# One core of Trainium2: the low half of the queries times the high half of the keys alone, as two 64-partition products

## The chip, the core and the metric

The kernel runs on one core of one Trainium2 chip, in one launch. The metric is the device time of that core in microseconds, lower is better. A run's time is the median of several executions; the profile is one further execution, recorded by the hardware profiler.

## The reference, cut to what matters

One layer of a hybrid decoder trunk over 2048 positions of width 1024: a modulated RMS norm, one combined projection `W_in` whose columns feed three groups of heads, an output projection with a residual, and a convolutional feed-forward block (1024 to 2 x 2816 to 1024) with another. One of the three groups is attention with a forget bias, 8 heads of 64; the others are a chunkwise mLSTM and a spatial gating unit. The change touches the scores of the attention alone:

```python
qa = rms_norm(to_heads(q_a, N_ATTN_HEADS), g_q).transpose(0, 2, 1, 3)
ka = rms_norm(to_heads(k_a, N_ATTN_HEADS), g_k).transpose(0, 2, 1, 3)
...
for blk in range(s_len // Q_BLOCK):              # 16 blocks of 128 queries
    lo, hi = blk * Q_BLOCK, (blk + 1) * Q_BLOCK
    logits = (jnp.einsum('bhtd,bhsd->bhts', q[:, :, lo:hi], k[:, :, :hi]) * scale
              + F[:, :, lo:hi, None] - F[:, :, None, :hi])
    logits = jnp.where(mask, logits, -jnp.inf)
    p = jax.nn.softmax(logits, axis=-1)
    outs.append(jnp.einsum('bhts,bhsd->bhtd', p, v[:, :, :hi]))
```

All inputs and the output are float32.

## The kernel before

**Split numbers.** Products are taken in the type float32r. To come near float32 each operand is split into a high half (the value copied into float32r) and a low half (what that copy lost). Most products of the kernel are `mm3` (lines 53 to 56): high times high, high times low, low times high. The scores do it otherwise: a head has 64 features, so the 64 high and the 64 low features of the keys fill the 128 partitions of one tile, and one product over 128 partitions gives the query's one half times both halves of the key.

**Stages.** By the clock of the profiled execution, the norms, the projections and the mLSTM run until about 690 us, the attention from there to about 1140 us, the output projection and the feed-forward block after it. The first scores of head 0 lie beside the last products of the projections (`acc`, L54 to L56). While attention runs, the projections' results come back from DRAM scratch: `k_d` and `q_d` hold for each pair of heads a high and a low block of 128 features (two heads of 64) by 2048 positions.

**Attention.** `load_k(h)` fills the tile `kk` of a head: partitions 0 to 63 the high halves of its keys, 64 to 127 the low halves, each by one DMA of 64 rows of 8 KB (L157). The forget bias `nf` (broadcast to all partitions) and the values follow. `load_q(h, tb, tag)` loads for 512 queries two tiles: `q2[0]` holds the high halves twice (on partitions 0 to 63 and again on 64 to 127), `q2[1]` the low halves twice (L173).

`scores` runs over the four blocks of 128 queries in 512, and for each over its keys in parts of up to 1024, one PSUM tile `sp` each (two buffers). Each part is one or two blocks of up to 512 keys. For each block two products over 128 partitions add into the same place (L206): `q2[0]` with `kk`, which is high times high plus high times low, and `q2[1]` with `kk`, which is low times high plus low times low. In the last block of a row a product of an identity with a mask (L210, bf16) adds the causal mask. Then one DVE instruction (L212) adds the bias, takes the row's extreme into `nm` and writes the tile `L`; ACT takes the exponentials (L223), GpSimd scales the rows (L225 to L228).

`finish` turns the weights on TensorE, four tiles of 128 by 128 at a time (`tp`, L259), splits them on ACT (`phi`, L262) and DVE (`plo`, L263), and multiplies them with the values (`op`, L245 and L246); ACT copies the result out (L250).

**Order.** `phase` puts the score parts of one step of 512 queries beside the `finish` of the step before, some parts of one, some of the other. The framework then orders each engine's instructions itself, so that on TensorE score products stand among transposes and value products. Keys and values of the next head are asked for after the first of a head's four steps; the queries of a step one step ahead. All loads go through the queue of SP, in order. L393, which the prediction uses, is a small transpose of parameter rows at the start of the kernel.

**Counts.** A head has 40 blocks of keys (4 + 8 + 12 + 16 for the four steps), so 640 products of L206 in all, and 128 mask products.

Of the kernel before, what the change touches and what calls it, by code (L numbers as in the profile page):

```python
# [8 lines left out]
F32 = mybir.dt.float32  # L9
# [8 lines left out]
P = 128  # L18
# [15 lines left out]
def trunk(  # L34
# [7 lines left out]
    V, A, G, T = nc.vector, nc.scalar, nc.gpsimd, nc.tensor  # L42
    dma = nc.sync.dma_start
# [19 lines left out]
    k_d = dr.tile([NH // 2, 2, P, S], F32, name="k_d")  # L63
# [32 lines left out]
    identb = cst.tile([P, P], BF16, name="identb")  # L96
    V.tensor_copy(identb, ident)
    maskb = cst.tile([P, P], BF16, name="maskb")
# [52 lines left out]
    def load_k(h):  # L151
        tag, e = "kvA" if h == 0 else "kvB", slice(h % 2 * 64, h % 2 * 64 + 64)
        kk = pool.tile([P, S], F32R, name="kk", tag=tag)
        nf = pool.tile([P, S], F32, name="nf", tag=tag)
        vv = pool.tile([P, S // P, P], F32R, name="vv", tag=tag)
        for i in range(2):
            dma(kk[64 * i : 64 * i + 64].bitcast(F32), k_d[h // 2, i, e])  # L157
        dma(nf, nf_d[h : h + 1, :].broadcast_to([P, S]))
        kv[h] = kk, nf, vv

# [21 lines left out]
    def l_tile(h, tb, c, w):  # L182
        if h and (tb == 0 or (tb, c) == (2, 1)) or (h, tb, c) == (0, 2, 1):
            tag = "L2"
        else:
            n_l[0] += 1
            tag = "LA" if h < NH - 2 and (n_l[0] - 1) % 20 < 8 else "LB"
        return pool.tile([P, w], F32, name="L", tag=tag)

    def scores(h, tb, q2, rows):  # L190

        kk, nf, _ = kv[h]
        for i in range(4):
            n_s = (tb * 4 + i + 1) * P
            parts = [(s0, min(1024, n_s - s0)) for s0 in range(0, n_s, 1024)]
            qs = slice(i * P, (i + 1) * P)

            nm = pool.tile([P, 2], F32, name="nm", tag="nm")
            L = []
            for c, (s0, w) in enumerate(parts):  # L200
                sp = pp.tile([P, 1024], F32, name="sp", tag="sp")
                for b in range(0, w, 512):
                    bw = min(512, w - b)
                    last = s0 + b + bw == n_s
                    for n in range(2):
                        T.matmul(  # L206
                            sp[:, b : b + bw], q2[n][:, qs], kk[:, s0 + b : s0 + b + bw], start=n == 0, stop=n == 1 and not last
                        )
                    if last:
                        T.matmul(sp[:, w - P : w], identb, maskb, start=False, stop=True)  # L210
                L.append(l_tile(h, tb, c, w))
                V.tensor_tensor_reduce(  # L212
                    out=L[c], in0=sp[:, :w], in1=nf[:, s0 : s0 + w], scale=-1.0, scalar=3.0e38 if c == 0 else nm[:, 0:1],
                    op0=ALU.add, op1=ALU.min, accum_out=nm[:, c : c + 1],
                )
                yield
            rows.append(L)
            rs = pool.tile([P, 2], F32, name="rs", tag="rs")

            def exps(L=L, nm=nm, rs=rs):  # L220
                n = len(L)
                for c in range(n):
                    A.activation(L[c], L[c], AF.Exp, bias=nm[:, n - 1 : n], scale=-1.0, accum_out=rs[:, c : c + 1])  # L223
                if n == 2:
                    G.tensor_tensor(rs[:, 0:1], rs[:, 0:1], rs[:, 1:2], op=ALU.add)  # L225
                G.tensor_tensor(rs[:, 0:1], rs[:, 0:1], mone, op=ALU.pow)
                for t in L:
                    G.tensor_scalar(t, t, rs[:, 0:1], 1.0, op0=ALU.mult, op1=ALU.mult)  # L228

            exps()  # L230
# [38 lines left out]
    def phase(now, then, lead=0):  # L269

        rows = []
        sc, n_sc = iter(()), 0
        if now:
            sc, n_sc = scores(*now, kv.pop(now) if now in kv else load_q(*now, "qB"), rows), (4, 4, 8, 8)[now[1]]
            if now in order and now != order[-1]:
                nxt = order[order.index(now) + 1]
                kv[nxt] = load_q(*nxt, "qB")
        n_fin = sum(4 * (t[1] + 1) for t in then)
        fin = (u for t in then for u in finish(*t))
        done = 0  # L280
        for n in range(n_sc):
            next(sc)
            while done < (n + 1 - lead) * (n_fin - 5) // (n_sc - lead):
                next(fin)
                done += 1
        for _ in sc:
            pass
        for _ in fin:
            pass
        return now and [(*now, rows)]  # L290
# [471 lines left out]
    def use_qk(which):  # L762
        def go(tt, ps):
            sq = pool.tile([P, 512], F32, name="qsq", tag="sq")
            A.activation(sq, ps, AF.Square)
            ss = pool.tile([P, 8], F32, name="ss", tag="ss")
            V.tensor_reduce(ss, sq.rearrange("p (h d) -> p h d", h=8), axis=AX.X, op=ALU.add)
            V.tensor_scalar(ss, ss, 1.0 / 64, EPS, op0=ALU.mult, op1=ALU.add)
            rsqrt(ss, 8)

            def normal():
                n = pool.tile([P, 8, 64], F32, name="qn", tag="q2k")
                V.tensor_tensor(n, ps.rearrange("p (h d) -> p h d", h=8), bc(ss, 2, 64), op=ALU.mult)
                after(3, lambda: turn(tt, n))

            after(1, normal)

        def turn(tt, n):
            tp = tr_ps()
            for j in range(4):  # L780
                T.transpose(tp[:, j * P : (j + 1) * P], n[:, 2 * j : 2 * j + 2].rearrange("p e d -> p (e d)"), ident)
            g, d = (gq8, q_d) if which == "q" else (gk, k_d)
            hi = pool.tile([P, 512], F32R, name="qhi", tag="qhl")
            lo = pool.tile([P, 512], F32R, name="qlo", tag="qhl")
            A.activation(hi, tp, AF.Copy, scale=g)
            V.scalar_tensor_tensor(lo, tp, g, hi.bitcast(F32), op0=ALU.mult, op1=ALU.subtract)
            for e, t in enumerate((hi, lo)):
                dma(
                    d[:, e, :, tt * P : (tt + 1) * P].rearrange("h p t -> p h t"),
                    t.bitcast(F32).rearrange("p (h t) -> p h t", h=4),  # L790
                )

        return go
# [125 lines left out]
    def mlstm(qi):  # L919
# [133 lines left out]
    blocks = [  # L1053
        ([(C_KM, 256), (C_G, 16)], nat(use_km)),
        ([(C_QM, 256), (C_VM + 256, 256)], do_qo),
        ([(C_VM, 256)], nat(use_vm)),
        ([(C_US, 512)], nat(use_sgu)),
        ([(C_K, 512)], nat(use_qk("k"))),
        ([(C_Q, 512)], nat(use_qk("q"))),
        ([(C_V, 512)], nat(use_v)),  # L1060
    ]
# [9 lines left out]
    for n, (half, i) in enumerate(steps):  # L1071
# [7 lines left out]
        if n == len(steps) - 1:  # L1079
            while background:  # L1080
                if next(background[0], True):
                    background.pop(0)
            n_accs[0] = 2
            pool.close("proj_r")
            pp.close("proj_r")
            attention_open_right()

            load_k(0)
            first_rows = [], []
            first = [scores(0, tb, load_q(0, tb, "qA"), r) for tb, r in zip((1, 0), first_rows)]  # L1090
            load_v(0, (0, 1))
            background += first
# [23 lines left out]
    last = [(0, 1, first_rows[0]), (0, 0, first_rows[1])]  # L1116
    order = [(h, tb) for h in range(NH) for tb in (TBS if h == NH - 1 else (2, 3) if h == 0 else range(4))]
    for h in range(NH):
        for n, tb in enumerate(TBS if h == NH - 1 else (2, 3) if h == 0 else range(4)):
            if (h, n) == (NH - 2, 1):  # L1120
                pool.close("att_r")
                wout_open_right()
            if (h, n) == (NH - 2, 3):
                load_w(0)
            last = phase((h, tb), last, 3 if (h, n) == (0, 0) else 0)
            if n == 0 and h < NH - 1:
                load_k(h + 1)
                load_v(h + 1, range(4))
# [607 lines left out]
```

## Time and profile before

| | |
|---|---|
| time, median of 3 runs (lowest, highest) | 2624.97 us (2623.48, 2627.48) |
| the profiled execution's own time | 2626.13 us |
| its span | 2624.1 us |
| PE, PEld busy | 2537.4 us, 2101.5 us |
| DVE, ACT, POOL busy | 2004.4 us, 1274.2 us, 399.0 us |
| DMA | 379.58 MB, mean 145 GB/s |
| mean granted clock of TensorE | 0.992 |

Engines: PE is TensorE's matmul, PEld its weight load (overlaps PE), DVE VectorE, ACT ScalarE, POOL GpSimd, SP the engine whose queue issues the DMAs. L206 is line 206 of the kernel. The recorded ends of matmuls are modelled and lie behind the start of the next one, so a product's cost in a steady run is the distance of two starts and not its duration. A timeline row has start and duration in us, the engine, the line, the operation, result and operands, shapes, and in brackets the idle time before it with what ended it ("issue": nothing that the profile shows). A row of the grouped lines has the busy time in us and the mean duration in ns behind the first bar, the idle time before it with what ended it behind the second.

### The profile page before, as it was taken

Reading aid. Unit: us, or ns where it says so; the run is one execution under the profiler, and the core shown is the slowest. Engines: PE = TensorE matmul, PEld = TensorE weight load, DVE = VectorE, ACT = ScalarE, POOL = GpSimd, SP = SyncE. Lnnn points to the kernel's source line nnn. Section 1 sums busy time; section 2 is a strip of 40 time slices with the busy share of each in tenths; the row PEclk is TensorE's granted clock in tenths of the full one; section 3 lists DMA queues with packets and bytes.
Section 4 is the critical chain, followed back from the end, with each engine's and each line's share of the span. In section 5 each row is a group of like instructions: output and inputs, shape, how many; then the busy total and the mean of one; then the engine's idle time right before and its main releaser. Section 6 shows DMA issues by size and latency. Waiting matters only on the chain.

```text
span 2624.1 us, 36472 instructions
## 1 busy us (share of the span) xinstructions
PE 2537.4 (97%) x12521; PEld 2101.5 (80%) x12537; DVE 2004.4 (76%) x3438; ACT 1274.2 (49%) x2424; POOL 399.0 (15%) x532
## 2 busy tenths in 40 slices
PE   5999999999999999999989999999999999999999
PEld 4887878878787887777768888888888888888787
DVE  7856646455378888866769888888888887898797
ACT  4333334333278888854555444444444444444443
POOL 2012210032246656620000000000000000000000
PEclk9999999999999999999999999999999999999999
DMA  7564653334564445257723222246222227658533
GB/s 248 173 185 132 194 153 111 116 88 131 165 177 113 114 136 165 65 162 238 274 65 105 89 81 84 86 160 225 81 88 81 87 66 256 233 166 295 186 95 117
DMA packets 302592, 379.58 MB, mean 145 GB/s; under 512 B 31934, under 2 KB 194588, under 8 KB 300360
## 3 DMA queue, kind: packets, MB, share of 16 engines
q1 hardware_dynamic: 302408, 377.26, 45.4%
q8 instruction: 99, 1.62, 0.3%
q14 instruction: 85, 0.70, 0.1%
HBM read 276.44 MB, written 100.74 MB: 144 GB/s over the span
## 4 chain that ended last, share of the span: by engine, by line
PE 76%; DVE 10%; DMA 5%; ACT 3%; issue 3%; POOL 2%; SPq 1%; DVEq 0%; ACTq 0%; POOLq 0%
PE ub L56 10%; PE ub L55 10%; PE ub L54 10%; PE acc L54 5%; PE acc L56 5%; PE acc L55 5%; PE db L55 4%; PE db L56 4%; PE db L54 4%; PE sp L206 3%; PE tp L259 3%; PE wps L55 2%; PE wps L54 2%; PE wps L56 2%; PE op L245 2%
## 5 line engine op out<-in xcount | busy, mean ns | idle before, releaser
L54 PE MATMUL acc<-wh,hh 128*128 128x512 f32 (+2 forms) x768 | 288.2, 376 | 4.3 <-DVE ev L688 2.3
L54 PE MATMUL ub<-T,wsph 128*128 128x512 f32 x704 | 274.2, 390 | 5.8 <-ACT wsph L1348 5.8
L56 PE MATMUL acc<-wh,hl 128*128 128x512 f32 (+2 forms) x768 | 275.7, 362 | 0.8 <-DVE hl L563 0.5
L55 PE MATMUL acc<-wl,hh 128*128 128x512 f32 (+2 forms) x768 | 275.3, 360 | 0.3 <-DVE wl L593 0.3
L56 PE MATMUL ub<-T,wspl 128*128 128x512 f32 x704 | 273.7, 389 | 0.6 <-DVE wspl L1349 0.6
L55 PE MATMUL ub<-T,wsph 128*128 128x512 f32 x704 | 273.9, 389 | 0.0
L55 PE MATMUL db<-wspl,wsph 128*128 128x512 f32 x616 | 240.2, 390 | 2.6 <-DVE wspl L1480 2.6
L56 PE MATMUL db<-wsph,wspl 128*128 128x512 f32 x616 | 239.6, 389 | 0.0
L54 PE MATMUL db<-wsph 128*128 128x512 f32 x616 | 238.2, 389 | 0.3 <-ACT wsph L1479 0.3
L1348 ACT CAST wsph<-S 128x512 fp32r<-128x512 f32 x176 | 109.7, 623 | 227.7 <-PE ub L55 159.1
L263 DVE TENSOR_TENSOR plo<-tp,phi 128x512 fp32r<-128x512 f32 (+1 forms) x320 | 186.9, 607 | 31.6 <-ACT phi L262 29.4
L54 PE MATMUL ub<-B,wsph 128*128 128x512 f32 x528 | 207.1, 392 | 2.8 <-ACT wsph L1348 2.8
L56 PE MATMUL ub<-B,wspl 128*128 128x512 f32 x528 | 207.0, 392 | 0.7 <-DVE wspl L1349 0.7
L55 PE MATMUL ub<-B,wsph 128*128 128x512 f32 x528 | 206.8, 392 | 0.0
L223 ACT ACTIVATE L<-L,nm 128x1024 f32<-128x1024 f32 (+2 forms) x192 | 172.5, 902 | 35.7 <-DVE nm L212 34.4
L259 PE MATMUL tp<-ident,L 128*128 128x128 f32 x1088 | 177.0, 274 | 2.6 <-POOL L L228 0.8
L262 ACT CAST phi<-tp 128x512 fp32r<-128x512 f32 (+1 forms) x320 | 159.9, 520 | 40.5 <-PE tp L259 38.9
L206 PE MATMUL sp<-kk,q 128*128 128x512 f32 (+3 forms) x640 | 169.3, 375 | 3.2 <-DVE nm L212 2.2
L1479 ACT CAST wsph<-act 128x512 fp32r<-128x512 f32 x132 | 82.2, 623 | 178.9 <-PE db L55 161.0
L228 POOL TENSOR_SCALAR L<-L,rs 128x1024 f32<-128x1024 f32 (+2 forms) x192 | 167.2, 880 | 11.0
L54 PEld LDWEIGHTS acc<-wh,hh 128*128 128x128 f32 x768 | 147.1, 192 | 24.2 <-DVE ev L688 2.7
L56 PEld LDWEIGHTS acc<-wh,hl 128*128 128x128 f32 x768 | 146.0, 191 | 23.1 <-DVE hl L563 1.3
(339 smaller groups left out, 5936.2 us busy)
## 6 DMA issues: line engine op xcount, KB each, us to landing
w<-in_w_up_dram SPq DMA_DIRECT2D x88, 512.0 KB
wd<-in_w_down_dram SPq DMA_DIRECT2D x176, 256.0 KB
wa<-in_w_ada_dram SPq DMA_DIRECT2D x96, 256.0 KB
act_d<-yc SPq DMA_DIRECT2D x44, 512.0 KB
act<-act_d SPq DMA_DIRECT2D x44, 512.0 KB
wr<-in_w_in_dram SPq DMA_DIRECT2D x64, 256.0 KB
q<-q_d SPq DMA_DIRECT2D x128, 128.0 KB
hc_d<-hl SPq DMA_DIRECT2D x28, 512.0 KB
```

Source lines behind the costliest of these rows:

```text
L54: T.matmul(ps, lh, rh, start=start, stop=False, skip_group_check=resume)
L55: T.matmul(ps, lh, rl, start=False, stop=False, skip_group_check=resume)
L56: T.matmul(ps, ll, rh, start=False, stop=stop, skip_group_check=resume)
L206: T.matmul(sp[:, b : b + bw], q2[n][:, qs], kk[:, s0 + b : s0 + b + bw], start=n == 0, stop=n == 1 and not last)
L223: A.activation(L[c], L[c], AF.Exp, bias=nm[:, n - 1 : n], scale=-1.0, accum_out=rs[:, c : c + 1])
L228: G.tensor_scalar(t, t, rs[:, 0:1], 1.0, op0=ALU.mult, op1=ALU.mult)
L245: T.matmul(op[:, c0:], vv[:, j, :], hi[:, c0:], start=(j == 0), stop=False)
L259: T.transpose(tp[:, i * P : (i + 1) * P], rows[i][j // 8][:, (j % 8) * P : (j % 8 + 1) * P], ident)
L262: A.copy(hi[:, c0:], tp[:, c0:])
L263: V.tensor_tensor(lo[:, c0:], tp[:, c0:], hi[:, c0:].bitcast(F32), op=ALU.subtract)
L1348: A.copy(hi, src)
L1479: A.copy(hi, v)
```

## The change

Three things change, all for the product of the query's low half.

- The low half of the query is multiplied with the high half of the key alone. Low times low is no longer computed where a part has two blocks.
- So this product needs 64 partitions. Where a part has two blocks of keys, the first block's product uses partitions 0 to 63 and the second's 64 to 127. For this the key tile is stored otherwise: in every odd block of 512 keys the low half lies on partitions 0 to 63 and the high half on 64 to 127. The product with `q2[0]`, which holds the high half on both, gives the same sum in either order. `load_k` takes four DMAs for it instead of two, each of 64 rows with two runs of 2 KB. A part with a single block keeps its product over 128 partitions.
- The order within a part: the first products of both blocks, then the mask, then the second products.

In the built program 256 of the 640 products run on 64 partitions (128 on each half), declared as products of a 64 by 128 part of the array; the other 384 and all else stay at 128 by 128.

```diff
@@ load_k
+        halves = lambda t: t.rearrange("p (a b c) -> p a b c", b=2, c=512)
         for i in range(2):
-            dma(kk[64 * i : 64 * i + 64].bitcast(F32), k_d[h // 2, i, e])
+            for b in range(2):
+                dma(halves(kk[64 * i : 64 * i + 64].bitcast(F32))[:, :, b, :], halves(k_d[h // 2, i ^ b, e])[:, :, b, :])
@@ scores
                 sp = pp.tile([P, 1024], F32, name="sp", tag="sp")
-                for b in range(0, w, 512):
-                    bw = min(512, w - b)
-                    last = s0 + b + bw == n_s
-                    for n in range(2):
-                        T.matmul(
-                            sp[:, b : b + bw], q2[n][:, qs], kk[:, s0 + b : s0 + b + bw], start=n == 0, stop=n == 1 and not last
-                        )
-                    if last:
-                        T.matmul(sp[:, w - P : w], identb, maskb, start=False, stop=True)
+                blocks = [(b, min(512, w - b)) for b in range(0, w, 512)]
+                last = s0 + w == n_s
+                for b, bw in blocks:
+                    T.matmul(sp[:, b : b + bw], q2[0][:, qs], kk[:, s0 + b : s0 + b + bw], start=True, stop=False)
+                if last:
+                    T.matmul(sp[:, w - P : w], identb, maskb, start=False, stop=False)
+                for n, (b, bw) in enumerate(blocks):
+                    r = slice(64 * n, 64 * n + 64) if len(blocks) == 2 else slice(0, P)
+                    T.matmul(sp[:, b : b + bw], q2[1][r, qs], kk[r, s0 + b : s0 + b + bw], start=False, stop=True)
```

## The prediction

> **What bounds the kernel now.** I read the page first, for the bound of the whole span, then the attention stage alone, since only it changes. The products of L206 run from 694.5 us to 1134.0 us (durations, then first and last start); I take 690 to 1140 us as the stage.
>
> ```profile
> L206 PEld LDWEIGHTS sp<-kk,q x640: 186/188/247, 694.5 to 1133.8; 128*128 128x128 f32 x160
> L206 PE MATMUL sp<-kk,q x640: 218/393/504, 694.7 to 1134.0; 128*128 128x512 f32 x127, 128*128 128x128 f32 x17, 128*128 128x384 f32 x16
> ```
>
> The page:
>
> ```profile
> span 2624.1 us, 36472 instructions
> PE 2537.4 (97%) x12521; PEld 2101.5 (80%) x12537; DVE 2004.4 (76%) x3438; ACT 1274.2 (49%) x2424; POOL 399.0 (15%) x532
> PE 76%; DVE 10%; DMA 5%; ACT 3%; issue 3%; POOL 2%; SPq 1%; DVEq 0%; ACTq 0%; POOLq 0%
> ```
>
> TensorE is busy for 97% of the span and carries 76% of the chain that ended last. In the stage, the windows view (span of the window, then busy time of PE, PEld, DVE, ACT, POOL, then the granted clock) and the grouped lines of PE say the same:
>
> ```profile
> 45.00:48.00 3.00, 2.70 (x10) 1.96 (x10) 2.97 (x9) 2.11 (x4) 1.99 (x4) 0.50 1.00 403
> 690.00:1140.00 450.00, 437.95 (x2614) 354.27 (x2612) 362.54 (x726) 345.52 (x757) 255.01 (x388) 1.00 0.47 132
> ```
>
> ```profile
> L259 PE MATMUL tp<-ident,L 128*128 128x128 f32 x1065 | 172.9, 274 | 1.9 <-DVE plo L263 0.6 <-POOL L L228 0.2
> L206 PE MATMUL sp<-kk,q 128*128 128x512 f32 (+3 forms) x640 | 169.3, 375 | 3.2 <-DVE nm L212 2.2
> L245 PE MATMUL op<-phi,vv 128*128 128x512 f32 (+2 forms) x309 | 131.0, 424 | 5.1 <-ACT yo L250 4.7 <-ACT phi L262 0.2
> ...
> L54 PE MATMUL acc<-wh,hh 128*128 128x512 f32 x49 | 19.4, 395 | 1.2 <-DVE vhl L759 1.2
> ```
>
> PE works in 438 of 450 us at the full clock (1.00), DVE in 363, ACT in 346. PE stands idle for 1.9 + 3.2 + 5.1 + 1.2 = 11.4 us. So a microsecond more or less of TensorE time in this stage moves the end by about a microsecond, until some 75 us less (438 against 363) would make DVE the bound. The first row, at half clock (0.50), is used below.
>
> **What a product costs.** The recorded time of a matmul holds a tail that overlaps the next. The cost is the distance of two starts:
>
> ```profile
> 1500.10 0.39 PE L55 MATMUL ub<-T,wsph 128*128 128x512 f32 x1
> 1500.10 0.19 PEld L56 LDWEIGHTS ub<-T,wspl 128*128 128x128 f32 x1
> 1500.32 0.39 PE L56 MATMUL ub<-T,wspl 128*128 128x512 f32 x1
> ```
>
> 512 columns cost 0.23 us (0.22 to 0.23 by these rounded starts), and the weights of the next product are loaded while this one streams (PEld starts with it), so a load costs nothing in a steady run. The shapes of L206 differ in their mean durations (last number before the bar's end):
>
> ```profile
> L206 PE MATMUL sp<-kk,q 128*128 128x512 f32 x448 | 138.3, 408 | 2.1 <-DVE nm L212 1.5
> ...
> L206 PE MATMUL sp<-kk,q 128*128 128x384 f32 x64 | 17.3, 351 | 0.3
> ...
> L206 PE MATMUL sp<-kk,q 128*128 128x256 f32 x64 | 14.1, 291 | 0.7 <-DVE nm L212 0.7
> L206 PE MATMUL sp<-kk,q 128*128 128x128 f32 x64 | 12.3, 254 | 0.1
> ```
>
> Taking those differences off 0.228 us: 384 columns cost 0.171, 256 cost 0.111, 128 cost 0.074 us.
>
> **Gain: two products in one time.** Of the 640 products 256 become 64-partition ones, 128 on partitions 0 to 63 and 128 on 64 to 127. In the order in which the built program hands them to TensorE, 110 pairs stand side by side: 71 of 512 with 512 columns, 16 of 512 with 384, 15 of 512 with 256, 7 of 512 with 128, one of 128 with 256. The other 18 pairs are taken apart by transposes and value products, up to 21 of them; these same places held other work between the same products before, so nothing is new in that. If a pair side by side runs in the time of its longer product, it saves the shorter: 71 x 0.228 + 16 x 0.171 + 15 x 0.111 + 8 x 0.074 = 21.2 us. The 18 split pairs save nothing. If the second product of a pair only starts after its own exposed load (0.11 us, below), the 71 equal pairs lose that again (7.8 us) and the 16 pairs with 384 about 0.05 each (0.9 us). I take the middle, a gain of 17 us, with 12.5 and 21.2 as ends.
>
> The TensorE page of the Trainium skill ("TensorE: Matmul & The Clock Gate", Part 3: Packing small matmuls) has products on different row groups start about 4 ns apart. By it the pairs would save 21.2 us less 110 x 0.004, as an estimate 20.8 us. No row of this trace shows two such products.
>
> **Loss: changing the row split of the array.** Each run of 64-partition products stands between full products. There are 110 runs of two and 36 of one, 146 runs, 292 changes. The attention stage of before has none. The trace has only three products on 32 partitions or fewer, those of L393, and one stands in a dense stream:
>
> ```profile
> 45.66 0.60 PE L56 MATMUL acc<-wh,hl 128*128 128x272 f32 x1 [0.30 <-DMA xt<-in_x_dram]
> 46.19 0.28 PE L393 MATMUL mp<-ident,rows 16*128 16x16 f32 x1
> 46.40 0.59 PE L54 MATMUL acc<-wh,hh 128*128 128x272 f32 x1
> 46.80 0.43 PE L55 MATMUL acc<-wl,hh 128*128 128x272 f32 x1
> 47.02 0.46 PE L56 MATMUL acc<-wh,hl 128*128 128x272 f32 x1
> ```
>
> ```profile
> 46.19 0.18 PEld L393 LDWEIGHTS mp<-ident,rows 16*128 16x128 f32 x1 [0.24 <-issue]
> 46.40 0.29 PEld L54 LDWEIGHTS acc<-wh,hh 128*128 128x128 f32 x1
> 46.57 0.33 PEld L55 LDWEIGHTS acc<-wl,hh 128*128 128x128 f32 x1
> ```
>
> The load for the 16-partition product is held for 0.24 us by nothing that the profile shows, and begins at 46.19, 0.07 before the recorded end (45.66 + 0.60 = 46.26) of the full product ahead. The next full load begins at 46.40, again 0.07 before the end (46.47) of the 16-partition product. Between two full products no load waits like that: L55's starts at 46.57, 0.42 before L54's end. So I read: where the row split changes, the next load waits until the array has nearly run empty, both ways, and is then exposed.
>
> At the full clock I price one change from two rows. A 512-column product is recorded for 0.39 us; a load 0.07 before that end comes at 0.32 instead of a next start at 0.23: 0.09 us. An exposed load is seen after an idle stretch:
>
> ```profile
> 702.99 0.73 PE L206 MATMUL sp<-kk,q 128*128 128x512 f32 x2 [0.16 <-DVE nm L212]
> 702.99 0.19 PEld L206 LDWEIGHTS sp<-kk,q 128*128 128x128 f32 x1 [0.30 <-DVE nm L212]
> ```
>
> Load and product start together, and two products take 0.73 us where the second is 0.39 long: it started 0.34 after the first, not 0.23, so 0.11 us. One change costs 0.09 + 0.11 = 0.20 us, and 292 of them 58.4 us. The lower end: the whole detour at half clock, halved. L56's successor was due 0.40 after it (as L54's came: 46.40 to 46.80), at 46.06, and came at 46.19 (0.13); the 16-partition product held the array 0.21; L54's own load cost 0.40 less the steady 0.22, 0.18. That is 0.52 us, about 0.50 for the two changes alone; half is 0.25 per run, 36.5 us in all. The upper end: nothing of it shrinks with the clock, 146 x 0.50 = 73 us. I keep 58.4, because both its parts use full-clock durations.
>
> "TensorEngine Tiling (Array Packing)" of the Trainium skill, section Tiling Modes, speaks against this change: it says that changing the tiling mode, not just the tile, drains the TensorE. The 16-partition rows agree with it. The TensorE page's drain of about 175 ns (Part 2, Single matmul latency) would make 292 changes cost 51 us, an estimate from that page alone.
>
> **The rest.** Order: both first products, then the mask, then the second products; the mask was last before. It is the same number of products and the row reduce of L212 waits for the last of them either way: nothing, hidden under no cover, since no step is added. Pairs that end later hold DVE back by the 0.2 to 0.4 us that PE itself is late, which is in the sum. Key loads: 32 issues instead of 16, of half the size.
>
> ```profile
> L157 SPq DMA_DIRECT2D kk<-k_d x16: 506/595/1435, 680.8 to 1019.5; - x16
> ```
>
> Two more issues per head at 595 ns put 1.2 us ahead of the bias, value and query loads on SP's queue. A head's keys are asked for three phases ahead, and the first (680.8 us) 13.7 us ahead of the first score (694.5), beside the last projection's products; without that cover it would be 1.2 us once. I take 0. The keys come in runs of 2 KB instead of 8 KB, while the stage moves 132 GB/s at 0.47 of the DMA engines' time; bounds 0 and, for the first head, another 1 to 2 us. PE's idle 11.4 us could take up some of the loss, where it waits for DVE and ACT that now catch up; most of it (L245 behind the copy of L250) is a loop through PE's own result. Ends 0 and 11.4, taken 4.
>
> **Sum** against the profiled execution of 2626.1 us (span 2624.1 and 2.0 around it, 1.2 above the median 2625.0): 58.4 - 17 - 4 = +37.4, so 2663.5, and 2662.4 from the median. I predict 2663.
>
> **The rivals.** *No pairing* (drains, but the two products of a pair follow each other): no gain, 58.4 - 4 = +54, 2680, up to 2699 with the 73. For it: no row shows two products at once. Against it: they use different partitions, different loads and different halves of the tile sp. *No drain* (ends faster): the load of L393 at 46.19 was held by something else in a crowded start, where the DMA engines were busy throughout (1.00 in the window of 45 to 48 us) and the clock halved; then loads of the other row split are pulled ahead like any others, and the pairs' gain stands alone: -17 to -21.2, about 2607. It decides below 17 / 292 = 0.06 us per change. Against it: the same 0.07 us on both sides of that product. *Neither* (the 64-partition products act as full ones, no pairing and no drain): the change then does not do what it says, 2625.
>
> **How the numbers follow.** Drain with pairing 0.62, no pairing 0.20, no drain 0.13, neither 0.05. The first case reaches from 36.5 - 21.2 - 11.4 = +3.9 (2630) to 73 - 12.5 = +60 (2687). The range 2630 to 2692 holds it and the greater part of the no-pairing case, and leaves out the last two (0.18). A measurement of this kernel tells some 0.2%, 5 us, from no change: faster 0.13, same 0.05, slower 0.82.
>
> **What would show it.** Right: the loads of the second products, and of whatever follows them, begin some 0.07 us before the recorded end of the product ahead and stand as idle "issue" on PEld; paired products start less than 0.12 us apart; the stage is 37 us longer and the rest of the span as long as before. Wrong: loads of 64-partition products start with the product ahead (no drain); pairs start 0.23 apart (no pairing); PE waiting for DVE, ACT or keys for tens of microseconds (another bound).

## The result and the profile after

The changed kernel takes 2643.6 us (median of 4, 2637.3 to 2648.5) where the kernel before takes 2625.8 (median of 4): a ratio of 1.0070 (95% interval 1.0055 to 1.0085), so 14 to 22 us slower. The forecast was 2663. Direction and range held; the size did not: +18 where +37 was forecast.

The page of the profiled execution (2647.3 us, among the longer of its runs):

```profile
span 2645.4 us, 36482 instructions
PE 2563.5 (97%) x12537; PEld 2085.6 (79%) x12537; DVE 2007.5 (76%) x3438; ACT 1277.7 (48%) x2424; POOL 398.7 (15%) x532
PE 80%; DVE 8%; DMA 6%; issue 2%; ACT 1%; POOL 1%; SPq 1%; DVEq 0%; ACTq 0%; POOLq 0%
```

PE carries 80% of the chain that ended last, 76% before; DVE, ACT and POOL gave that up. The last value product shows where the time went (line views: durations, first and last start; L246 is before, L248 and L207 after):

```profile
L246 PE MATMUL op<-plo,vv x320: 272/394/487, 737.2 to 1147.0; 128*128 128x512 f32 x128, 128*128 128x256 f32 x32
```

```profile
L248 PE MATMUL op<-plo,vv x320: 273/396/487, 741.1 to 1164.8; 128*128 128x512 f32 x128, 128*128 128x256 f32 x32
L207 PE MATMUL sp<-kk,q x320: 218/397/505, 696.3 to 1151.4; 128*128 128x512 f32 x128, 128*128 128x128 f32 x16, 128*128 128x384 f32 x16
```

From the first score (694.7 before, 696.3 after) to the last value product are 452.3 us before and 468.4 after: 16.2 us in the stage. Another 1.6 us lie ahead of it and some 3 us after it in this execution; where these come from was not followed. The median's +18 is nearer to the stage alone. The wait that stood out in the stage, value products waiting for ACT's copy (5.1 us idle at L245, 4.7 of it for L250), is gone, here in the grouped lines of PE (L247 is the old L245):

```profile
L247 PE MATMUL op<-phi,vv 128*128 128x512 f32 x224 | 102.4, 457 | 0.5 <-ACT yo L252 0.2
L248 PE MATMUL op<-plo,vv 128*128 128x512 f32 x224 | 94.2, 421 | 0.0
L207 PE MATMUL sp<-kk,q 128*128 128x512 f32 x224 | 82.7, 422 | 1.7 <-DVE nm L214 1.1
L212 PE MATMUL sp<-kk,q 64*128 64x512 f32 x208 | 68.3, 496 | 0.0
```

Now a pair in the timeline of PE, then of PEld (mask L209, second products L212, transposes L261):

```profile
871.14 0.23 PE L209 MATMUL sp<-maskb,identb 128*128 128x128 bf16 x1
871.30 0.50 PE L212 MATMUL sp<-kk,q 64*128 64x512 f32 x2
871.73 0.44 PE L261 MATMUL tp<-ident,L 128*128 128x128 f32 x2
```

```profile
871.30 0.19 PEld L212 LDWEIGHTS sp<-kk,q 64*128 64x128 f32 x2
871.73 0.31 PEld L261 LDWEIGHTS tp<-ident,L 128*128 128x128 f32 x3 [0.24 <-DVE nm L214]
```

Both mechanisms are there as forecast. Two products of 512 columns take 0.50 us together, as one does: in the trace their starts are 3 ns apart. And the load that follows begins at 871.73, 0.07 before the recorded end at 871.80; the load of the pair itself begins at 871.30, 0.07 before the mask's end at 871.37. (The row puts the wait ahead of the transposes' load down to DVE. But the same distance stands where it names nothing: at each of the 146 places where a run of 64-partition products begins, the new load comes 0.07 us before the recorded end of the product ahead.) So the 0.07 that stood at half clock in the trace of before holds at full clock.

### The profile page after: what moved, and what is told of

Its sections match the earlier page's. It is cut to its first block, busy times and chain, and to the rows that moved or that the text cites. A ratio compares the mean times of both kernels' runs of the same rounds, so it can differ in the third digit from the quotient of the medians.

```text
span 2645.4 us, 36482 instructions
## 1 busy us (share of the span) xinstructions
PE 2563.5 (97%) x12537; PEld 2085.6 (79%) x12537; DVE 2007.5 (76%) x3438; ACT 1277.7 (48%) x2424; POOL 398.7 (15%) x532
## 4 chain that ended last, share of the span: by engine, by line
PE 80%; DVE 8%; DMA 6%; issue 2%; ACT 1%; POOL 1%; SPq 1%; DVEq 0%; ACTq 0%; POOLq 0%
PE ub L56 10%; PE ub L55 10%; PE ub L54 10%; PE acc L54 5%; PE acc L56 5%; PE acc L55 5%; PE tp L261 5%; PE db L55 4%; PE db L56 4%; PE db L54 4%; PE sp L207 3%; PE sp L212 2%; PE op L247 2%; PE op L248 2%; DMA wa<-in_w_ada_dram 2%
## 5 line engine op out<-in xcount | busy, mean ns | idle before, releaser
L261 PE MATMUL tp<-ident,L 128*128 128x128 f32 x1088 | 179.5, 278 | 1.8 <-POOL L L230 1.2
L261 PEld LDWEIGHTS tp<-ident,L 128*128 128x128 f32 x1088 | 128.8, 140 | 44.4 <-issue 16.6
```

The costliest lines, as they stand in the source:

```text
L261: T.transpose(tp[:, i * P : (i + 1) * P], rows[i][j // 8][:, (j % 8) * P : (j % 8 + 1) * P], ident)
```

## The experiments

Two theories went into them, numbered as in the expectations. **Theory 1, the price is not paid in full in this stage**: a change costs its 0.2 us, but part of that fills time in which TensorE stood still anyway. **Theory 3, the price is too high**: a change costs half of what was read from one place. Two side causes were to be told apart from both: the new order of the products (theory 2), and the new loads. A steady distance is the time from one start to the next in a dense stretch: 0.227 us for a product of 512 columns.

### The order alone

```diff
-                    r = slice(64 * n, 64 * n + 64) if len(blocks) == 2 else slice(0, P)
+                    r = slice(0, P)          # and load_k as before
```

> The new order of the products alone: both first products of a part, the mask, then both second products, all on 128 partitions, keys loaded and stored as before. Theory 1 (the price of a change of the row split is right, and PE's waits for the other engines swallow a part of it): no change, 2623 to 2628. Theory 2 (the changes cost what was priced, but the new order itself gives time back, because the mask no longer stands last): 8 to 12 us faster than before, 2614 to 2618. Theory 3 (a change costs less than priced): no change.

Measured 2625.7 us, ratio 1.0001 (0.9992 to 1.0010). The order gives and costs nothing. Its trace is the control for what follows, since its products stand in nearly the order of the changed kernel.

### The loads alone

```diff
-        for i in range(2):
-            dma(kk[64 * i : 64 * i + 64].bitcast(F32), k_d[h // 2, i, e])
+        # the four DMAs of the changed kernel; scores as before
```

> The new storage of the keys alone (four DMAs a head in runs of 2 KB, odd blocks low half first), products and order as before. Forecast: 0 to 2 us, 2625 to 2628. If the loads are what makes the changed kernel's runs spread wider (2637 to 2648), they spread here as well.

Measured 2627.5 us, ratio 1.0003 (0.9994 to 1.0012), runs from 2621.4 to 2632.6: no cost that can be measured. The runs spread over 11 us, those of the new order alone over 9 (2621.9 to 2631.0), so the loads are not shown to be what spreads the changed kernel's.

### No pairing

```diff
-                    r = slice(64 * n, 64 * n + 64) if len(blocks) == 2 else slice(0, P)
+                    r = slice(0, 64) if len(blocks) == 2 else slice(0, P)   # load_k as before
```

> Both second products of a pair on partitions 0 to 63, keys loaded and stored as before: every change of the row split stays, the pairing goes. If the pairs run side by side in the changed kernel (its trace has the two starts 2 ns apart), this costs the 21 us that the pairing saves on top of its 18: 2660 to 2666. If waits still swallow more than half of what is added, 2651 to 2655.

Measured 2659.0 us, ratio 1.0130 (1.0113 to 1.0147): 33.7 us over before, 15.4 over the changed kernel. That is somewhat under the forecast. The 145 runs of this kernel have no pairing gain, so at 0.40 us each they should have cost 58 us; they cost 34.

The same place in the control and in this kernel (timelines of PE; mask L207, second products L210, transposes L259):

```profile
859.41 0.23 PE L207 MATMUL sp<-maskb,identb 128*128 128x128 bf16 x1
859.45 0.71 PE L210 MATMUL sp<-kk,q 128*128 128x512 f32 x2
860.00 0.38 PE L259 MATMUL tp<-ident,L 128*128 128x128 f32 x2
```

```profile
872.70 0.23 PE L207 MATMUL sp<-maskb,identb 128*128 128x128 bf16 x1
872.86 0.73 PE L210 MATMUL sp<-kk,q 64*128 64x512 f32 x2
873.52 0.44 PE L259 MATMUL tp<-ident,L 128*128 128x128 f32 x2
```

From the mask to the second transpose (0.27 before the end of the last row) are 0.70 us in the control, 0.99 without pairing, and 0.76 in the changed kernel (871.14 to 871.90). The steady distances (mask 0.067, twice 0.227, transpose 0.109) add up to 0.63. So the control has 0.06 us too much already: the mask product is so short that it does not hide the next load, and two second products take 0.71 us, the first 0.32 of them (859.45 to 859.77). And a transpose behind a run shows only 0.06 us of its load (second start 0.17 after the first, not 0.11), where a product of 512 columns shows 0.11.

I made this sum for each run whose neighbours stand alike in both traces (141 of 145, starts of the trace). A run costs 0.382 us over the steady distances: 0.34 in the commonest case (behind the mask, ahead of a transpose), 0.42 between products. The control has 0.076 over the steady distances at the same places. So 0.307 a run is added, 43.3 us, and everywhere else the stage is 10 us shorter, 33.3 in all. (The stage here is the time from the first score to the last value product.)

### More runs

```diff
-                    r = slice(64 * n, 64 * n + 64) if len(blocks) == 2 else slice(0, P)
+                    r = slice(64 * n, 64 * n + 64)
```

> The changed kernel, and also the 64 single products of the parts with one block on 64 partitions (low times low is left out there too): some 64 more runs of 64-partition products, with no pairing gain. At the price of 0.40 us a run, with the idle time already used up (theory 1): 64 x 0.40 = 26 us, less about 0.05 for each run that ends at a transpose, so 22 to 26 us over the changed kernel, 2665 to 2670. If a fixed share of every change is swallowed, or a change costs half of what was priced (theory 3): 10 to 13 us, 2653 to 2657.

Measured 2654.8 us, ratio 1.0109 (1.0094 to 1.0124): 29.4 over before, 11 over the changed kernel, 0.17 us for each of 64 runs. This is what I had expected of theory 3. But the trace reads otherwise. One added run stands at a 2.1 us wait in both kernels; the other 63 cost 0.384 us each over the steady distances, and the changed kernel already had 0.140 over them at the same places. That adds 15.5 us, and the stage is 15.1 longer. The next experiment takes the price where there is little to swallow it.

### The price where TensorE does not wait

```diff
@@ Down.mm, for block i of 4 at each of 154 steps
-                mm3(self.ps[p][i], ah[:, sl], al[:, sl], bh, bl, not more and k == 0, k == KH - 1, resume=more)
+                ps, r, skip = self.ps[p][i], slice(0, 64) if i == 0 else slice(0, P), dict(skip_group_check=more)
+                T.matmul(ps, ah[:, sl], bh, start=not more and k == 0, stop=False, **skip)
+                T.matmul(ps, ah[r, sl], bl[r], start=False, stop=False, **skip)
+                T.matmul(ps, al[:, sl], bh, start=False, stop=k == KH - 1, **skip)
```

> The price by itself, in a stretch where TensorE hardly ever waits: in the down projection one product in twelve (high times low of the first of four blocks, at each of 154 steps) runs on partitions 0 to 63 alone, between full products; it leaves out the other half of that product's sum. Attention is as before. At 0.40 us a run: 154 x 0.40 = 62 us slower than before, 2685 to 2690. At half that (theory 3): 31 us.

Measured 2681.9 us, ratio 1.0214 (1.0197 to 1.0231): 56 us, 0.365 a run. The timeline of PE, a run of one between full products:

```profile
2302.60 0.39 PE L1497 MATMUL db<-wsph 128*128 128x512 f32 x1
2302.91 0.50 PE L1498 MATMUL db<-wspl,wsph 64*128 64x512 f32 x1
2303.34 0.50 PE L1499 MATMUL db<-wsph,wspl 128*128 128x512 f32 x1
2303.68 0.39 PE L1497 MATMUL db<-wsph 128*128 128x512 f32 x1
```

The three starts are 0.31, 0.43 and 0.34 us apart (median 0.318, 0.428, 0.333) instead of three times 0.227: 0.398 us over, where the prediction had 0.40. The price of a change was right to 2%. That 154 of them cost 56 and not 61 us fits the 3.9 us that the starts of this stretch lay over the steady distances before; here nothing is over them but the runs. Theory 3 falls.

Two products a run, on both halves (i = 0 on partitions 0 to 63, i = 1 on 64 to 127, issued next to each other):

> The same stretch, two products side by side on the two halves of the partitions at each of 154 steps (high times low of the first two of four blocks, half of each sum left out). One product's time (0.227 us) is saved a step: 154 x (0.404 - 0.227) = 27 us slower than before, 2650 to 2654. If pairs did not run side by side: 62 us.

Measured 2650.6 us, ratio 1.0100 (1.0084 to 1.0115): 25 us, as forecast.

Four products a run (all four blocks, halves in turn):

> The same stretch, four products in one run at each step, on the two halves in turn (half of each of these sums left out). Two products' time is saved a step: 154 x (0.404 - 0.454) = 8 us faster than before, 2616 to 2620: a run pays from four products on. If the second pair of a run does not start beside or right behind the first, slower than before by up to 27 us.

Measured 2627.0 us, ratio 1.0006 (0.9997 to 1.0016): the 8 us did not come. The timeline of PE shows a run (L1500):

```profile
2301.82 0.73 PE L1500 MATMUL db<-wspl,wsph 64*128 64x512 f32 x4
2302.48 0.50 PE L1502 MATMUL db<-wsph,wspl 128*128 128x512 f32 x1
```

Four products end after 0.73 us, so the second pair (recorded for 0.39) starts 0.34 us after the first. Its loads are not exposed, though. The timeline of PEld has all four loads of the run done by 2302.12, before the second pair starts at 2302.15:

```profile
2301.82 0.30 PEld L1500 LDWEIGHTS db<-wspl,wsph 64*128 64x128 f32 x4 [0.36 <-DVE wspl L1480]
```

What shows in the 0.34 is the first pair's own load: product and load are recorded from the same moment. In return the full product behind the run starts 0.32 us after the second pair, where it starts 0.43 after a single pair. From the full product ahead to the second one behind, a run of four takes 1.318 us and a run of two 1.088 (medians), so the second pair costs 0.230, one steady product. A whole run of four therefore saves 0.044 us, 6.6 us for the 151 that the framework left whole. In the other three steps it put work between the four, and the nine shorter runs there cost 3.3 us. That leaves 3 us of the 8; the measured +1.4 (-0.8 to +4.2) is still some 5 us above that, and where these went is not shown. By its starts a run of four pays a little; in the kernel's time it broke even.

### The mask last again

```diff
-                if last:
-                    T.matmul(sp[:, w - P : w], identb, maskb, start=False, stop=False)
                 for n, (b, bw) in enumerate(blocks):
...
+                if last:
+                    T.matmul(sp[:, w - P : w], identb, maskb, start=False, stop=True)
```

> The changed kernel with the mask product last again, behind the second products: the load that is exposed where a run ends is then often the mask's bf16 load (96 ns recorded) and not a float32 one (140 to 190 ns), and the load behind it is pulled ahead. Forecast: 2 to 6 us faster than the changed kernel, 2638 to 2642; if the load's kind does not matter, the same as the changed kernel.

Measured 2638.7 us, ratio 1.0049 (1.0034 to 1.0064), about 5 us less than the changed kernel by the medians; the intervals overlap a little. In the traces the stage is 1.8 us shorter (466.6 against 468.4). It fits the forecast, is no proof, and is slower than before all the same.

### Work added without a change of the row split, and work taken away

```diff
+                if w > 512:
+                    T.matmul(sp[:, 0:512], q2[0][:, qs], kk[:, s0 : s0 + 512], start=True, stop=True)   # once, or twice
                 for b in range(0, w, 512):
```

> How much of added TensorE time the attention swallows when no row split changes: the kernel before, and in each of the 128 parts with two blocks the first product (512 columns, 128 partitions) is issued once more ahead of itself, into the place that it writes anyway. That adds 128 x 0.227 = 29 us of steady TensorE time. If the stage has some 45 us of gaps on TensorE that shrink as its work grows (read from the traces as the stage's length less its products times their steady distances), about half is swallowed: 12 to 18 us slower, 2637 to 2643. If TensorE has no slack and it is the changes of the row split that are cheaper here than in the down projection: 27 to 29 us, 2652 to 2655.

Measured 2659.4 us, ratio 1.0133 (1.0120 to 1.0146): 35 us for 29 us of work. By the traces the stage is 29.1 us longer, just its work; the other 6 us lie outside it.

> The same with two more, 58 us of steady TensorE time, about what 145 runs of 64-partition products cost at the price of the down projection. With gaps that shrink: 30 to 38 us slower, 2655 to 2663, as with both products on one half (2659). Without: 54 to 58 us, 2679 to 2684.

Measured 2676.2 us, ratio 1.0198 (1.0185 to 1.0211): 52 us for 58 (in the stage 50.3). Both miss what I expected. In both the framework also planned another order of score products, transposes and value products, and what that did wasn't separated. With this reserve they speak against the idea that TensorE's stage has 45 us of slack that any added work could use: some 7 of 58 us were swallowed here, about what went away elsewhere in the kernel without pairing (10).

> What a free pairing could have given: the new order, all on 128 partitions, and in each part with two blocks the second product of the second block (query's low half) is left out, so that block lacks those two terms. 128 products less, 71 to 85 of 512 columns and the rest shorter: about 25 us of steady TensorE time. If the end followed TensorE's time one for one: 2600 to 2604. If the gaps grow as its work shrinks, at the rate at which they shrank: 8 to 14 us faster, 2612 to 2618.

```diff
-                for n, (b, bw) in enumerate(blocks):
-                    r = slice(64 * n, 64 * n + 64) if len(blocks) == 2 else slice(0, P)
-                    T.matmul(sp[:, b : b + bw], q2[1][r, qs], kk[r, s0 + b : s0 + b + bw], start=False, stop=True)
+                T.matmul(sp[:, : blocks[0][1]], q2[1][:, qs], kk[:, s0 : s0 + blocks[0][1]], start=False, stop=True)
+                # load_k as before; the stop flags of the other products follow
```

Measured 2619.5 us, ratio 0.9981 (0.9971 to 0.9990): 25 us of TensorE work less, and only 5 us gained (3 to 8; in the stage 8.5), a little short of the lower forecast. The grouped lines of PE in the stage (L258 transposes, L206 first products):

```profile
L258 PE MATMUL tp<-ident,L 128*128 128x128 f32 x1088 | 176.1, 275 | 8.1 <-POOL L L227 4.7 <-DVE plo L262 2.3
...
L206 PE MATMUL sp<-kk,q 128*128 128x512 f32 (+2 forms) x320 | 106.5, 388 | 6.4 <-DVE nm L211 5.4
```

PE now waits for GpSimd's scaling and DVE's reduce and split. The stage's length less its steady work grew from 45 us to 61 by the starts. But this run, too, has an order of its own: some 370 of its 2503 products in the stage stand elsewhere in the sequence than in the control, about as many as moved with two products more. Whether the missing work or the other order makes PE wait wasn't separated. So it is a hint, and not shown, that a pairing free of any price would have brought far less than the 25 us that it takes off TensorE.

## Why the prediction was right or wrong

**Right: where the row split changes, the next load waits and is exposed.** Read from one 16-partition product at half clock, it holds at full clock: 0.07 us before the recorded end, on both sides. The price of 0.20 us per change is 0.199 in the down projection. "TensorEngine Tiling (Array Packing)" of the Trainium skill (Tiling Modes) says that a change of the tiling mode, and not of the tile alone, drains TensorE. This trace agrees: the next product comes 0.32 us after a full one of 512 columns where the mode changes, and 3 ns after the first of a pair, where only the half does.

**Right: the pairs run in one time.** Forecast 17 us, ends 12.5 and 21.2; between the kernel without pairing and the changed one the runs differ by 0.143 us on average, 20 us, in the time by 15. The second product's load is not exposed within a pair; taking the middle was too careful. "TensorE: Matmul & The Clock Gate" of the Trainium skill (Part 3: Packing small matmuls) has packed products start about 4 ns apart. Here they start 3 ns apart.

**Right: order and loads at nothing.** Neither shows a cost clear of the noise (1.0001 and 1.0003).

**Wrong: that every change pays its full price in this stage, and that PE had only 11.4 us to give, of which I took 4.** This is the step that failed: the 58.4 us of the changes were set against steady distances, as if nothing stood at those places before. In the stage's 146 runs:

| term | forecast, us | by the traces, us |
|---|---|---|
| changes of the row split, over steady distances | 58.4 | 146 x 0.382 = 55.8 |
| excess that stood at the same places already (control) | 0 | -146 x 0.076 = -11.1 |
| pairing | -17 | -142 x 0.143 = -20.3 |
| waits elsewhere that went away | -4 | 14.1 - 23.2 = -9.1 |
| sum | +37.4 | +15.3 |

(The last term is the stage against the control, +14.1, less what the 142 runs that can be matched add, 142 x 0.163 = 23.2. Read directly, the distances outside the runs shrink by 9.6 us. The median's +18 lies some 2.5 above that sum.) Between the two sums lie 22 us: 11.1 stood at the very places where runs were put, 5.1 more than the 4 taken went away elsewhere, 3.3 is the better pairing and 2.6 the slightly cheaper change.

Of the 11 us, 3.6 stand at 58 runs behind the mask, where the short mask product had left the next load exposed all along. Another 3.9 stand at seven places where a value product waited for ACT's copy, and the rest, some 3.5 us, is spread over the other runs. Of what went away elsewhere, 3.3 us is the same wait at five more places (from 0.83 to 0.17 us between two starts). So this wait, 4.7 us in the idle column before (4.6 in the control), held some 7 us by the control's starts. I called it a loop through PE's own result and kept it; it went.

The bound of 11.4 us was itself misread. The idle column counts from a product's recorded end, which lies about 0.16 us behind the moment when the next could have started. Every gap shorter than that is invisible in it. The stage's starts against the steady distances show 45 us of gaps before, four times as much. The experiments with added work speak against taking those gaps for slack that anything can use. And with 25 us of TensorE work less, the stage was only 8.5 us shorter, so the prediction's microsecond for a microsecond did not hold downwards in that run.

**The rivals.** *No pairing*, *no drain* and *neither* are all refuted by the starts in the trace. The no-drain case was priced at -17 to -21; that 25 us of work less brought 5 makes this price doubtful, with the reserve made there about the order.

## What to carry to other kernels

Two products on the two halves of the partitions do run in one product's time, but a run of them pays about 0.2 us to begin and 0.2 to end, so with 512 columns (0.227 us) it takes four products a run to about break even, and a single pair among full products loses. Price an added stall against what stands at the same place already, by distances of starts and not by the idle column. And before pricing a gain on the busiest engine, look at how near the next ones are: here 25 us off TensorE were worth 5, in a run whose order had changed as well.

## What was not expected of the hardware

A 128-column bf16 product is too short to hide the float32 load behind it: the product after the mask comes 0.039 us behind it but holds the array 0.313, together 0.06 more than the steady 0.067 and 0.227. And where a load is exposed, a single distance of starts misleads. In a run of four products on two halves the second pair starts 0.332 us after the first and not 0.227, though its loads were done by then; the 0.105 more is the first pair's own load, and the distance behind the second pair is shorter by as much (0.323 and not 0.428). Only the sum over the whole run tells what the pair costs.
